# LayerNorm at the planner's lowest rank, its weight and bias folded into the transposed copy for the next layer, and another order of the first transfers

## The chip, the cores and the metric

The kernel runs on one core of one Trainium2 chip. The metric is the device time of one execution in microseconds (us); lower is better. The core has five engines that each work through an instruction queue of their own in order: TensorE (PE in the profile, with its weight loads as PEld), VectorE (DVE), ScalarE (ACT), GpSimd (POOL) and SyncE (SP, which here only issues DMAs). ACT issues a few DMAs too.

## The reference, cut to what matters

Two decoder layers over a sequence of 2048 tokens and 1024 channels, float32. Layer 0 mixes tokens with a gated delta rule (8 heads), layer 1 with gated linear attention (4 heads); each is followed by a residual and a LayerNorm:

```python
for i in range(DEPTH):                       # DEPTH = 2
    y = gdn_mixer(x, ...) if i % 2 == 0 else gla_mixer(x, ...)
    x = layer_norm(DEEP_ALPHA * x + y, ln_g[i], ln_b[i])

def layer_norm(x, g, b):
    mu = mean(x, -1); xc = x - mu; var = mean(xc * xc, -1)
    return xc * rsqrt(var + LN_EPS) * g + b
```

A mixer is an input projection (`x @ w_in`, 1024 by 6160 or by 3088), work per head and per chunk of tokens, a gated norm, and an output projection (`o @ w_out`, 2048 or 1024 by 1024). In layer 0 the gate and conv work is part of it. All products are wanted at float32 accuracy.

## The kernel before

**Tiling.** Tokens are cut into four groups of 512 (`TG`); a group is four tiles of 128 tokens (`NC = 4`, index n). A *unit* is one head of one layer for one group. `PHASES` gives the order of groups: layer 0 of groups 0 and 1, layer 1 of group 0, layer 0 of group 2, layer 1 of group 1, layer 0 of group 3, layer 1 of groups 2 and 3. That makes 48 units: eight for each of the four layer 0 groups (some 70 us each), four for each of the four layer 1 groups (some 55 us each).

**A unit's stages.** `gemms` multiplies the transposed input of the group (tiles xh, xl, read as xraw) with the unit's columns of the input weights; every float32 product is three fp32r products of high and low parts. `preps` does the work inside chunks, `chains` the recurrence over the four tiles, and `outs` multiplies the head's result (tiles oth, otl) with the output weights (tile wo) into PSUM buffer pso, of which there is one, and adds it to the residual: tile y, [128 tokens x 1024], with only four buffers, so one group's y at a time. After a group's last head `layer_norm` runs on each of the four y tiles: statistics on DVE (lnst, lnmv), the inverse root on POOL (lnrs), normalising on ACT (y<-y,lnmr,lnrs), multiplication with the weight on DVE and addition of the bias on POOL (both y<-y,gb), and a store, to x2 in layer 0 and to out in layer 1. In layer 0 the finished y is also transposed by PE (psg<-cst,y), copied from PSUM by ACT (xraw<-psg) and stored as x2T (x2T<-xraw, on ACT's queue); layer 1 later loads x2 as its residual (y<-x) and x2T as its transposed input (xraw<-x2T). The tile xraw has four buffers, shared between these loads and stores.

**Weights.** `chunk` brings one [128 x 256] piece of an input weight. At its first use it is loaded raw (wraw<-in_w_in), split in high and low part (wc; the high part by ACT, the low part by POOL), used, and the split pair is stored to DRAM (wk<-wc). At each later use the pair is loaded (wc<-wk). `load_wo` does the same for output weights (woraw, wo, wok), with ACT and DVE splitting. So the first eight units, and the first four of layer 1, load raw and store; all others only load.

**What sets the order.** Nothing runs as it is written. A `Recorder` notes every operation with its rank and unit. `place` then simulates the engines with a table of costs and lags, in which DMA issues are one more engine: whenever an engine is free it takes, of the operations that are ready by the simulation and whose buffers are free, the one with the lowest (rank, place in the program). Ranks before the change, first to last: `R_CHAIN`, `R_PREP`, `R_OUT`, `R_GEMM`, `R_SETUP`. An operation that needs a new buffer waits until its unit is at most two ahead of the first with an unfinished chain (`HORIZON`). The result is emitted as fixed instruction queues; on the chip each engine keeps that order, and an instruction whose data is late holds up all behind it. Since `emit` (line 356) issues everything, nearly every row of the profile says L356, and operations are told apart by tiles.

**Lines that the change touches.** `Recorder.cost` (a DMA issue is charged 430 ns on its queue, 520 for wc and wk), `chunk` and `load_wo`, `outs`, `load_gb` and `layer_norm`, the list of ranks, and the host's layout of inputs. In `outs` the loads of y and, through `load_wo`, of woraw have rank `R_OUT`, which stands ahead of `R_GEMM`:

```python
def outs(u):
    rec.rank = R_OUT
    if u.first:
        u.G["y"] = load_y(...)
```

Of the kernel before, what the change touches and what calls it, by code (L numbers as in the profile page):

```python
# [7 lines left out]
F32 = mybir.dt.float32  # L8
# [115 lines left out]
class Recorder:  # L124
# [53 lines left out]
    def cost(self, op, dst, every):  # L178
        key = op.key
        n = size_of(dst.shape)  # L180
        psum = any(isinstance(a, View) and a.of.psum for a in every)
        op.func = None
        if key == "t":
            mov = size_of(every[2].shape) if op.name == "matmul" else size_of(every[1].shape)
            if op.name == "transpose":
                op.cost = 2 * dst.shape[0] / 2.4 + 4
            elif every[1].dtype == F32:
                op.cost = 4 * mov / 2.4 + 9
            else:
                op.cost = mov / 2.25 + 4.5  # L190
            op.lag = 210
            op.func = op.name == "matmul" and min(dst.shape[0], every[1].shape[0]) < P
        elif key == "d":
            size = 4 * n * dst.shape[0]
            tag = dst.of.tag if isinstance(dst, View) else ""
            op.cost, op.lag = 520 if tag == "wc" or tag[:2] == "wk" else 430, DMA_LAG + size / 170
            if tag == "Arep":
                op.cost, op.lag = 620, REP_LAG
        elif key == "a":
            size = 4 * n * dst.shape[0]  # L200
            op.cost, op.lag = 340, DMA_LAG + size / 170
        elif key == "v":
            n = max(n, max(size_of(a.shape) for a in every))
            took = (150 if psum else 160) + 1.04 * n
            if op.name in ("tensor_reduce", "copy_predicated", "tensor_tensor_scan"):
                took += 1.0 * n
            if op.name != "tensor_tensor" and any(isinstance(a, (View, bass.AP)) and size_of(a.shape) == 1
                                                  for a in every[1:]):
                took += 62 if psum or n < 512 else 85
            op.cost, op.lag = took - 80, 80 + LAG  # L210
        elif key == "s":
            took = (165 if psum else 210) + 0.833 * n
            if any(isinstance(op.kw.get(k), (View, bass.AP)) for k in ("scale", "bias")):
                took += 100 + 67 * ("scale" in op.kw and "bias" in op.kw)
            if "accum_out" in op.kw:
                took += 190
            if op.name == "activation":
                op.func = "ln" if op.args[2] == AF.Ln else None if op.args[2] in (AF.Copy, AF.Square, AF.Identity,
                                                                                 AF.Abs) else "exp"
            op.cost, op.lag = took - 95, 95 + LAG  # L220
        else:
            took = 140 + 2.8 * n if len(every) > 2 else 185 + n
            if op.args[-1] == ALU.pow:
                took = 450 + 160 * n
            op.cost, op.lag = took - 40, 40 + LAG
# [148 lines left out]

@with_exitstack
def trunk(ctx, tc, x, xT, w_in1, conv, a_log, dt_bias, nw1, w_out1, w_in2, gk_up, gk_b, nw2, w_out2,
          ln_g, ln_b, consts, out, phases=None):
    nc = tc.nc
    rec = Recorder()
    v, s, g = (rec.engine(e, k) for e, k in ((nc.vector, "v"), (nc.scalar, "s"), (nc.gpsimd, "g")))  # L380
# [50 lines left out]
    nws = [T(f"nw{k}", [P, 2]) for k in range(2)]  # L431
    gkb = T("gkb", [P, H2])
    mhalf = T("mhalf", [P, NC])
    up = T("up", [80, 512], dt=F32R)
    halo = T("halo", [P, 32, 3])
    S1 = [T(f"S1_{h}", [P, DV]) for h in range(H1)]
# [22 lines left out]
    def setup_gla():  # L459
        sync.dma_start(nws[1][:], nw2)  # L460
        v.tensor_scalar(nws[1][:], nws[1][:], NORM, None, ALU.mult)
        sync.dma_start(gkb[:], gk_b)
        raw = T("th", [P, 512], 2)
        v.memset(raw[:], 0.0)
        for r0 in (0, 32, 64):
            sync.dma_start(raw[r0:r0 + 16, :], gk_up)
        s.copy(up[:], raw[:80, :])
        v.tensor_tensor(up[64:80, :], raw[64:80, :], up[64:80, :].bitcast(F32), ALU.subtract)
# [27 lines left out]
    def chunk(spec):  # L496


        w, cols, kc, key = spec
        wc = T("wc", [P, 2, 272], W_BUFS, F32R)  # L500
        n = sum(2 * cn if pair else cn for c0, cn, pair in cols)
        if key in kept:
            sync.dma_start(wc[:, :, :n].bitcast(F32), kept[key][:])
            return wc
        raw = T("wraw", [P, 272], RAW_BUFS)
        rows = w[kc * P:(kc + 1) * P]
        n = 0
        for c0, cn, pair in cols:
            if pair:
                sync.dma_start(raw[:, :2 * cn].rearrange("p (a b) -> p a b", a=2),  # L510
                               rows[:, :2 * pair].rearrange("p (a b) -> p a b", a=2)[:, :, c0:c0 + cn], also=(wc,))
                n = 2 * cn
            else:
                sync.dma_start(raw[:, n:n + cn], rows[:, c0:c0 + cn], also=(wc,) if n == 0 else ())
                n += cn
        split(wc[:, 0, :n], wc[:, 1, :n], raw[:, :n], g)
        kept[key] = T("wk", [P, 2, n], p=dr)
        sync.dma_start(kept[key][:], wc[:, :, :n].bitcast(F32))
        return wc

    def load_wo(spec, parts=None):
# [11 lines left out]
        if key in kept_wo:  # L533
            sync.dma_start(t[:].bitcast(F32), kept_wo[key][:])
        else:
            for j in range(2):
                raw = T("woraw", [P, 512], WO_RAW_BUFS)
                r0 = h * DV + j * P
                sync.dma_start(raw[:], w_out[r0:r0 + P, e * 512:(e + 1) * 512], also=(t,) if j == 0 else ())
                s.activation(t[:, j, 0, :], raw[:], AF.Copy, scale=nw[:, j:j + 1])  # L540
                v.scalar_tensor_tensor(t[:, j, 1, :], raw[:], nw[:, j:j + 1], t[:, j, 0, :].bitcast(F32),
                                       ALU.mult, ALU.subtract)
            kept_wo[key] = T("wok", [P, 2, 2, 512], p=dr)
            sync.dma_start(kept_wo[key][:], t[:].bitcast(F32))
# [461 lines left out]
    def outs(u):  # L1006
        rec.rank = R_OUT
        if u.first:
            u.G["y"] = load_y((lambda n: x[u.t0 + n * P:u.t0 + (n + 1) * P, :]) if u.kind == 0
                              else (lambda n: x2[u.gi][n][:]))  # L1010
        ys = u.G["y"]
        end = u.at + 1 == len(units)
        wo = {}
# [3 lines left out]
        for e, n in [(e, n) for n in range(NC) for e in range(2)] if end else [(e, n) for e in range(2) for n in range(NC)]:  # L1017
            final = u.last and e
            if e not in wo:
                wo[e] = load_wo(u.wo_specs()[e])  # L1020
            if final and not n and not end:
                gb = load_gb(u)
            c = slice(e * 512, (e + 1) * 512)
            d = PS("g" if u.at + 2 >= len(units) else "o", [P, 512])
            for j in range(2):
# [2 lines left out]
            y = ys[n]  # L1028
            v.scalar_tensor_tensor(y[:, c], d, u.z[:, n:n + 1], y[:, c], ALU.mult, ALU.add)
            if final:  # L1030
                layer_norm(u, n, y, gb)
        if u.last and u.kind == 0:
            for n in range(NC):
                for q in range(2):
                    d = PS("g", [P, 4, P])
                    transposes(d, lambda i: ys[n][:, (4 * q + i) * P:(4 * q + i + 1) * P], 4)
                    xt = T("xraw", [P, 4, P], X_RAW_BUFS)
                    s.copy(xt[:], d)
                    acts.dma_start(x2T[u.gi][:, 4 * q:4 * q + 4, n * P:(n + 1) * P], xt[:])

    def load_gb(u):
        gb = []
# [4 lines left out]
                gb.append(t)  # L1047
        return gb

    def layer_norm(u, n, y, gb):  # L1050
        st, mv = T("lnst", [P, 2, 6], 2), T("lnmv", [P, 2], 2)
        rs, mr = (small(k, 1, LN_BUFS) for k in ("lnrs", "lnmr"))
        for e in range(2):
            v.bn_stats(st[:, e, :], y[:, e * 512:(e + 1) * 512])
        v.bn_aggr(mv[:], flat(st[:]))
        rsqrt(rs[:], mv[:, 1:2], 1e-5 / ALPHA ** 2)
        v.scalar_tensor_tensor(mr[:], mv[:, 0:1], -1.0, rs[:], ALU.mult, ALU.mult)
        dst = x2[u.gi][n] if u.kind == 0 else out[u.t0 + n * P:u.t0 + (n + 1) * P, :]
        end = u.at + 1 == len(units)
        for e in range(2):  # L1060
            c = slice(e * 512, (e + 1) * 512)
            s.activation(y[:, c], y[:, c], AF.Identity, scale=rs[:], bias=mr[:])
            v.tensor_tensor(y[:, c], y[:, c], gb[e][:], ALU.mult)
            (v if end and n == NC - 1 else g).tensor_tensor(y[:, c], y[:, c], gb[2 + e][:], ALU.add)
            sync.dma_start(dst[:, c], y[:, c])

    for u in units:
# [10 lines left out]
WO_BUFS, WO_RAW_BUFS = 2, 2  # L1078
LN_BUFS = 4
N_WARM = 5  # L1080
R_CHAIN, R_PREP, R_OUT, R_GEMM, R_SETUP = range(5)
HORIZON = 2
LAGS_C = (0, 3)
LAGS_T = (0, 3, 8, 11)
# [3 lines left out]
def host_layout(np, i):  # L1088
# [15 lines left out]
        "w_out2": f(np.asarray(i["gla_w_out"])[0]),  # L1104
        "ln_g": f(np.asarray(i["ln_g"])),
        "ln_b": f(np.asarray(i["ln_b"])),
        "consts": shape_constants(np),
    }

# [16 lines left out]
```

## Time and profile before

| what | us |
|---|---|
| median of 3 runs | 3136.71 (3135.39 to 3137.48) |
| the profiled execution, its own time | 3134.49 |
| span of that execution, first to last instruction | 3132.6 |
| PE busy | 3026.9 (97%) |
| DVE busy | 2041.2 (65%) |
| ACT busy | 1174.5 (37%) |
| POOL busy | 520.1 (17%) |
| granted TensorE clock, mean | 0.987 |

The profile lists one execution. A row of the timeline or of the groups gives the engine, the operation, the tile it writes and those it reads (out<-in), shapes, and how often (x4). A timeline row begins with start and duration; its bracket holds the idle time of the engine ahead of it and what ended that. A row of the windows view is one stretch of time: the busy time of each engine with its count of instructions, the granted clock of PE, the share of the DMA engines and GB/s. Times that the texts call span plus 1.9 us (3134.49 less 3132.6) are the profiled execution's own.

### The profile page before, as it was taken

The page shows a single profiled execution, that of the slowest core. Times are in us where ns is not written, and L with a number is a line of the kernel's source. Part 1 is how long each engine was busy: PE and PEld are TensorE (multiplying, and loading weights), DVE is VectorE, ACT ScalarE, POOL GpSimd, SP SyncE. Part 2 cuts the span into 40 slices and gives each one's busy share as a digit, 9 for nine tenths or more (in the row PEclk, how much of TensorE's full clock was granted, in tenths as well). Part 3 has the DMA queues.
Part 4 walks back from the last instruction along what each step waited for, and adds up shares of the span by engine and source line. Part 5 has one row for each costly group of instructions (what it writes and reads, how often), then busy time and mean ns, then how long its engine had stood idle before and what let it go on. Part 6 is the DMA issues. An engine that isn't in the chain of part 4 may idle for free.

```text
span 3132.6 us, 51373 instructions
## 1 busy us (share of the span) xinstructions
PE 3026.9 (97%) x18430; PEld 2592.1 (83%) x18430; DVE 2041.2 (65%) x4780; ACT 1174.5 (37%) x3091; POOL 520.1 (17%) x834
## 2 busy tenths in 40 slices
PE   7999999999999989999999999999999999999997
PEld 5788888788888878888888888998888889889886
DVE  5777777766666675576675667447666666646645
ACT  4544444433223454443332344323333334423422
POOL 3433332200000243320000002002000000201001
PEclk9999999999999999999999999999999999999999
DMA  8766567654555558674445445547444544655542
GB/s 268 222 194 216 179 213 232 190 169 125 153 176 155 177 182 265 208 234 151 128 145 177 145 157 188 162 157 238 137 142 141 156 147 146 212 172 180 175 142 91
DMA packets 442479, 551.85 MB, mean 176 GB/s; under 512 B 37568, under 2 KB 381888, under 8 KB 430192
## 3 DMA queue, kind: packets, MB, share of 16 engines
q1 hardware_dynamic: 416112, 530.74, 53.6%
q10 hardware_dynamic: 26112, 17.83, 2.0%
q8 instruction: 145, 2.38, 0.3%
q14 instruction: 110, 0.90, 0.1%
HBM read 421.24 MB, written 127.21 MB: 175 GB/s over the span
## 4 chain that ended last, share of the span: by engine, by line
PE 80%; DVE 9%; DMA 5%; ACT 3%; issue 2%; POOL 1%; SPq 1%; ACTq 0%; DVEq 0%; POOLq 0%
PE psg L356 45%; PE psc L356 15%; PE pso L356 14%; PE psh L356 6%; DMA wraw<-in_w_in 2%; DVE y L356 2%; DVE acc L356 1%; ACT junk L356 1%; DVE D L356 1%; SPq L356 1%; POOL wc L356 1%; DMA x2T<-xraw 1%; DVE lnst L356 1%; DVE kd L356 1%; DVE Xt L356 0%
## 5 line engine op out<-in xcount | busy, mean ns | idle before, releaser
L356 PE MATMUL psg<-xh,wc 128*128 128x512 f32 x2560 | 902.4, 416 | 13.8 <-ACT xh L356 7.3
L356 PE MATMUL psg<-wc,xh 128*128 128x256 f32 (+1 forms) x4096 | 809.1, 290 | 19.5 <-ACT wc L356 13.1
L356 PEld LDWEIGHTS psg<-wc,xh 128*128 128x128 f32 x4096 | 656.4, 190 | 45.2 <-ACT wc L356 15.2
L356 PE MATMUL psg<-wc,xl 128*128 128x256 f32 (+1 forms) x2048 | 589.5, 290 | 0.0
L356 PEld LDWEIGHTS psg<-xh,wc 128*128 128x128 f32 x2560 | 480.8, 190 | 112.2 <-ACT xh L356 9.1
L356 PE MATMUL psg<-xl,wc 128*128 128x512 f32 x1280 | 532.9, 417 | 0.5 <-DVE xl L356 0.5
L356 PE MATMUL pso<-wo,oth 128*128 128x512 f32 x1472 | 477.0, 403 | 17.1 <-DVE y L356 16.3
L356 DVE SCALAR_TENSOR_TENSOR y<-pso,z,y 128x512 f32<-128x512 f32 x368 | 274.4, 746 | 194.4 <-PE pso L356 171.5
L356 PEld LDWEIGHTS psg<-wc,xl 128*128 128x128 f32 x2048 | 388.8, 191 | 7.1
L356 DVE SCALAR_TENSOR_TENSOR acc<-pb,taps,acc 128x512 f32<-128x512 f32 x384 | 300.0, 785 | 77.8 <-ACT acc L356 71.5
L356 PEld LDWEIGHTS pso<-wo,oth 128*128 128x128 f32 x1472 | 260.2, 189 | 75.8 <-DVE y L356 28.4
L356 POOL TENSOR_TENSOR wc<-wraw,wc 128x256 fp32r<-128x256 f32 (+1 forms) x288 | 233.2, 824 | 417.4 <-ACT wc L356 388.5
L356 PE MATMUL pso<-wo,otl 128*128 128x512 f32 x736 | 295.4, 401 | 0.1
L356 PEld LDWEIGHTS psg<-xl,wc 128*128 128x128 f32 x1280 | 243.2, 190 | 48.1 <-DVE xl L356 1.9
L356 ACT ACTIVATE th<-psg 128x256 f32<-128x256 f32 (+1 forms) x256 | 108.8, 437 | 447.2 <-PE psg L356 419.4
L356 ACT ACTIVATE junk<-psc 128x128 bf16<-128x128 f32 (+1 forms) x448 | 144.4, 322 | 226.4 <-PE psc L356 125.2
L356 POOL COPY halo<-pb 128x3 f32<-128x3 f32 x128 | 29.2, 228 | 902.3 <-ACT pb L356 900.0
L356 ACT COPY pb<-psg 128x512 f32<-128x512 f32 x128 | 74.9, 585 | 250.7 <-PE psg L356 237.7
L356 PEld LDWEIGHTS pso<-wo,otl 128*128 128x128 f32 x736 | 139.3, 189 | 30.6 <-DVE otl L356 0.9
L356 DVE SCALAR_TENSOR_TENSOR sg<-th,psg 128x256 f32<-128x256 f32 x192 | 79.9, 416 | 125.8 <-ACT th L356 111.6
L356 ACT CAST wc<-wraw 128x256 fp32r<-128x256 f32 (+1 forms) x288 | 110.0, 406 | 122.9 <-DMA wraw<-in_w_in 104.0
L356 ACT ACTIVATE D<-D 128x512 f32<-128x512 f32 x160 | 99.2, 630 | 115.5 <-DVE D L356 108.1
(171 smaller groups left out, 4391.4 us busy)
## 6 DMA issues: line engine op xcount, KB each, us to landing
wc<-wk SPq DMA_DIRECT2D x816, 256.0 KB, 3.5
wo<-wok SPq DMA_DIRECT2D x70, 1024.0 KB, 4.9
wk<-wc SPq DMA_DIRECT2D x272, 256.0 KB, 3.5
wraw<-in_w_in SPq DMA_DIRECT2D x288, 128.0 KB, 3.7
wok<-wo SPq DMA_DIRECT2D x24, 1024.0 KB, 6.1
Arep<-blk SPq DMA_DIRECT2D x32, 512.0 KB
wc<-wk SPq DMA_DIRECT2D x48, 272.0 KB, 3.2
woraw<-in_w_out SPq DMA_DIRECT2D x48, 256.0 KB, 4.4
```

What stands on the lines that cost most here:

```text
L356: tc.keep_in_program_order(op.call(*[real(a) for a in op.args], **{k: real(a) for k, a in op.kw.items()}))
```

## The change

1. A new rank `R_LN` stands between `R_GEMM` and `R_SETUP`. `layer_norm`, the loads of weight and bias (`load_gb`) and the new `affine` get it, but for the very last unit, where they keep `R_OUT`.
2. `layer_norm` now ends with the normalised y. Multiplication with the weight, addition of the bias and the store move to `affine`. In layer 1 it follows directly. In layer 0 the transposes read the y that is only normalised, and ACT applies weight and bias, which in the transposed tile are one number per partition (new input ln_T, tile lnT), in the copy from PSUM; `affine` on y follows behind the transposes.
3. The transposes of a group are ordered by channel block: four transposes (one per token tile, last tile first) fill one PSUM tile, and the store to x2T writes 512 consecutive tokens per partition rather than four blocks of 128.
4. The bias is added by DVE instead of POOL, but for the first three tiles of the last unit.
5. Loads of y get rank `R_GEMM` (`R_SETUP` in the first unit), those of woraw too.
6. The split input weights of the first two units (`N_UNKEPT = 2`) are not stored; the first two heads of the second group load them raw, split them again and store them.
7. The planner charges 480 ns for a DMA issue (630 for wc and wk, 560 for wraw, 720 for Arep), and 9500 ns until a load of y has landed.

```diff
@@ Recorder.cost
-            op.cost, op.lag = 520 if tag == "wc" or tag[:2] == "wk" else 430, DMA_LAG + size / 170
+            op.cost, op.lag = 630 if tag == "wc" or tag[:2] == "wk" else 560 if tag == "wraw" else 480, DMA_LAG + size / 170
             if tag == "Arep":
-                op.cost, op.lag = 620, REP_LAG
+                op.cost, op.lag = 720, REP_LAG
+            elif tag == "y":
+                op.lag = 9500
@@ setup_gla
+        sync.dma_start(lnT[:], ln_T)
@@ chunk
+        keep = rec.unit >= N_UNKEPT
...
-        kept[key] = T("wk", [P, 2, n], p=dr)
-        sync.dma_start(kept[key][:], wc[:, :, :n].bitcast(F32))
+        if keep:
+            kept[key] = T("wk", [P, 2, n], p=dr)
+            sync.dma_start(kept[key][:], wc[:, :, :n].bitcast(F32))
@@ load_wo
             for j in range(2):
+                rec.rank = R_GEMM if rec.unit else R_SETUP
                 raw = T("woraw", [P, 512], WO_RAW_BUFS)
                 r0 = h * DV + j * P
                 sync.dma_start(raw[:], w_out[r0:r0 + P, e * 512:(e + 1) * 512], also=(t,) if j == 0 else ())
+                rec.rank = R_OUT
@@ outs
         if u.first:
+            rec.rank = R_GEMM if u.at else R_SETUP
             u.G["y"] = load_y(...)
+            rec.rank = R_OUT
...
             if final and not n and not end:
+                rec.rank = R_LN
                 gb = load_gb(u)
+                rec.rank = R_OUT
...
             if final:
-                layer_norm(u, n, y, gb)
+                if not end:
+                    rec.rank = R_LN
+                layer_norm(u, n, y)
+                if u.kind:
+                    affine(u, n, y, gb)
+                rec.rank = R_OUT
         if u.last and u.kind == 0:
+            for kc in range(KC):
+                d = PS("g", [P, NC, P])
+                for n in reversed(range(NC)):
+                    pe.transpose(d[:, n, :], ys[n][:, kc * P:(kc + 1) * P], ident)
+                xt = T("xraw", [P, TG], X_RAW_BUFS)
+                s.activation(xt[:], flat(d), AF.Identity, scale=lnT[:, kc:kc + 1], bias=lnT[:, KC + kc:KC + kc + 1])
+                acts.dma_start(x2T[u.gi][:, kc, :], xt[:])
+            rec.rank = R_LN
             for n in range(NC):
-                for q in range(2):
-                    d = PS("g", [P, 4, P])
-                    transposes(d, lambda i: ys[n][:, (4 * q + i) * P:(4 * q + i + 1) * P], 4)
-                    xt = T("xraw", [P, 4, P], X_RAW_BUFS)
-                    s.copy(xt[:], d)
-                    acts.dma_start(x2T[u.gi][:, 4 * q:4 * q + 4, n * P:(n + 1) * P], xt[:])
+                affine(u, n, ys[n], gb)
@@ layer_norm
+        for e in range(2):
+            c = slice(e * 512, (e + 1) * 512)
+            s.activation(y[:, c], y[:, c], AF.Identity, scale=rs[:], bias=mr[:])
+
+    def affine(u, n, y, gb):
         dst = x2[u.gi][n] if u.kind == 0 else out[u.t0 + n * P:u.t0 + (n + 1) * P, :]
         end = u.at + 1 == len(units)
         for e in range(2):
             c = slice(e * 512, (e + 1) * 512)
-            s.activation(y[:, c], y[:, c], AF.Identity, scale=rs[:], bias=mr[:])
             v.tensor_tensor(y[:, c], y[:, c], gb[e][:], ALU.mult)
-            (v if end and n == NC - 1 else g).tensor_tensor(y[:, c], y[:, c], gb[2 + e][:], ALU.add)
+            (g if end and n < NC - 1 else v).tensor_tensor(y[:, c], y[:, c], gb[2 + e][:], ALU.add)
             sync.dma_start(dst[:, c], y[:, c])
@@ constants
+N_UNKEPT = 2
-R_CHAIN, R_PREP, R_OUT, R_GEMM, R_SETUP = range(5)
+R_CHAIN, R_PREP, R_OUT, R_GEMM, R_LN, R_SETUP = range(6)
```

More of the change, by code (lines that the diff above doesn't have):

```diff
@@ L376, in trunk @@
 def trunk(ctx, tc, x, xT, w_in1, conv, a_log, dt_bias, nw1, w_out1, w_in2, gk_up, gk_b, nw2, w_out2,
-          ln_g, ln_b, consts, out, phases=None):
+          ln_g, ln_b, ln_T, consts, out, phases=None):
     nc = tc.nc
@@ L433, in trunk @@
     mhalf = T("mhalf", [P, NC])
+    lnT = T("lnT", [P, 2 * KC])
     up = T("up", [80, 512], dt=F32R)
@@ L1048, in load_gb, with layer_norm @@
         return gb
-    def layer_norm(u, n, y, gb):
+    def layer_norm(u, n, y):
         st, mv = T("lnst", [P, 2, 6], 2), T("lnmv", [P, 2], 2)
@@ L1106, in host_layout @@
         "ln_b": f(np.asarray(i["ln_b"])),
+        "ln_T": f(np.stack([np.asarray(i["ln_g"])[0], np.asarray(i["ln_b"])[0]]).reshape(2 * KC, P).T),
         "consts": shape_constants(np),
```

## The prediction, made before the changed kernel was run

> **What bounds the kernel now.** I read the page first, for the busiest engine, then the windows in steps of 40 us, for where that engine rests, then the waits in the worst of them.
>
> ```profile
> span 3132.6 us, 51373 instructions
> PE 3026.9 (97%) x18430; PEld 2592.1 (83%) x18430; DVE 2041.2 (65%) x4780; ACT 1174.5 (37%) x3091; POOL 520.1 (17%) x834
> ```
>
> PE rests 3132.6 - 3026.9 = 105.7 us. Its work is not changed (the transposes are as many as before), so the change can win only these rests and what hangs on them. Columns below: stretch; PE, PEld, DVE, ACT, POOL busy (and instructions); PE's granted clock; DMA share; GB/s.
>
> ```profile
> 0.00:40.00 40.00, 25.99 (x89) 17.86 (x90) 20.06 (x39) 16.55 (x33) 11.95 (x21) 0.87 0.88 296
> 40.00:80.00 40.00, 32.40 (x168) 26.73 (x168) 21.49 (x48) 16.64 (x59) 20.53 (x28) 0.96 0.78 244
> 80.00:120.00 40.00, 37.43 (x201) 31.88 (x199) 34.74 (x74) 19.20 (x45) 22.76 (x32) 0.96 0.80 243
> 160.00:200.00 40.00, 39.52 (x264) 33.82 (x265) 25.75 (x75) 16.85 (x56) 11.75 (x19) 1.00 0.67 218
> ...
> 600.00:640.00 40.00, 34.70 (x208) 27.48 (x207) 34.48 (x76) 18.19 (x33) 16.87 (x22) 1.00 0.93 299
> 640.00:680.00 40.00, 39.94 (x238) 35.02 (x237) 27.72 (x80) 13.06 (x45) 2.66 (x5) 1.00 0.42 127
> ...
> 1120.00:1160.00 40.00, 33.79 (x195) 28.10 (x192) 35.03 (x59) 25.59 (x53) 24.51 (x26) 0.99 0.53 173
> 1160.00:1200.00 40.00, 32.61 (x199) 28.84 (x199) 20.26 (x45) 15.11 (x34) 6.16 (x8) 0.84 0.81 261
> ...
> 1360.00:1400.00 40.00, 36.49 (x153) 29.27 (x152) 30.98 (x73) 16.44 (x44) 17.21 (x23) 0.91 0.88 281
> ...
> 1920.00:1960.00 40.00, 35.13 (x216) 30.45 (x215) 24.13 (x45) 14.91 (x29) 7.07 (x5) 0.91 0.71 230
> ...
> 2120.00:2160.00 40.00, 36.56 (x155) 29.34 (x155) 30.84 (x73) 16.44 (x44) 17.95 (x23) 0.91 0.83 278
> ...
> 2680.00:2720.00 40.00, 34.89 (x216) 30.17 (x215) 23.80 (x45) 14.57 (x29) 8.02 (x7) 0.91 0.72 241
> ...
> 2880.00:2920.00 40.00, 37.24 (x238) 32.14 (x237) 32.23 (x65) 20.00 (x37) 14.35 (x13) 0.96 0.79 254
> ```
>
> The reader is to see that the rests lie together: at the start and at the seven places where a group ends in LayerNorm. A low clock follows each long rest and costs again; as its price I take 40 us times (1 - clock), an upper bound, since part of it falls on the rest itself. Rest plus clock:
>
> - start, three rows: 14.0 + 7.6 + 2.6 = 24.2 of rest, 5.2 + 1.6 + 1.6 = 8.4 of clock: 32.6
> - 600: 5.3
> - 1120 and 1160: 13.6 + 6.8 = 20.4
> - 1360 and 2120: 6.9 + 7.2 = 14.1
> - 1920 and 2680: 10.0 + 7.2 = 17.2
> - 2880: 2.8 + 1.6 = 4.4
>
> That is 94.0 in all, and 61.4 of it at the seven LayerNorms.
>
> **The start.** SP's issues (first three) and PE's first real product:
>
> ```profile
> 0.72 1.81 SPq L356 DMA_DIRECT2D y<-in_x  x4
> 2.58 0.95 SPq L356 DMA_DIRECT2D woraw<-in_w_out  x2
> 3.57 0.45 SPq L356 DMA_DIRECT2D xraw<-in_xT  x1
> ...
> 12.33 1.22 PE L356 MATMUL psg<-xh,wc 128*128 128x512 f32 x2 [6.32 <-ACT xh L356]
> ```
>
> Six DMAs that nobody needs for tens of us are issued ahead of the first input, 2.5 MB (4 x 512 KB, 2 x 256 KB). At the 296 GB/s of the first row they take 8.4 us. The new ranks put them behind: the first xraw goes out at 0.72 rather than 3.57 (2.85 us) and then has the DMA engines to itself. The head's gain lies between 2.85 and the whole wait of 6.32; I take 5.5, nearer the upper end, because the 8.4 us of transfer in front go too. These y and woraw loads, the constants and the new lnT (128 x 16 numbers, one more small DMA) still go out in unit 0, later.
>
> The other 24.2 - 6.3 = 17.9 us of rest up to 120 us are small waits, mostly for raw weights that arrive late at DMA shares of 0.78 to 0.88. The first two units lose their 48 stores (24 chunks each), 256 KB apiece: 12.6 MB of the 31.3 MB that the three rows moved (40 us x 296 + 244 + 243 GB/s). SP also saves 48 issues. Bounds: nothing, and 17.9. I take 7, since part waits for DVE or ACT in the first convolutions. With the rests, of 8.4 us of clock I take 3.5. Start: -16 (bounds -3 and -30).
>
> The price: two heads of the second group are loaded raw, split and stored again. Row 160 is such a stretch (first group), row 640 one that only loads; PE differs by 0.42 us in 40, so 140 us cost 1.5. I take +2.
>
> **LayerNorm.** What POOL's bias does, at the second group's end (timeline; then the groups):
>
> ```profile
> 1149.04 5.57 DVE L356 TENSOR_TENSOR y<-y,gb 128x512 f32<-128x512 f32 x4 [0.21 <-ACT y L356]
> 1150.63 6.77 POOL L356 TENSOR_TENSOR y<-y,gb 128x512 f32<-128x512 f32 x4
> 1154.53 3.41 DVE L356 SCALAR_TENSOR_TENSOR wo<-woraw,nw,wo 128x512 fp32r<-128x512 f32 x2
> 1159.78 1.09 PE L356 MATMUL psg<-cst,y 128*128 128x128 f32 x4 [5.40 <-POOL wc L356]
> ```
> ```profile
> L356 POOL TENSOR_TENSOR y<-y,gb 128x512 f32<-128x512 f32 x62 | 94.9, 1550 | 26.4 <-DVE y L356 13.2 <-PE psg L356 6.1 <-issue 4.1
> L356 DVE TENSOR_TENSOR y<-y,gb 128x512 f32<-128x512 f32 x66 | 57.6, 898 | 1.1 <-ACT y L356 0.8
> L356 DVE SCALAR_TENSOR_TENSOR wo<-woraw,nw,wo 128x512 fp32r<-128x512 f32 x48 | 39.3, 833 | 3.9 <-ACT wo L356 3.9
> L356 ACT ACTIVATE y<-y,lnmr,lnrs 128x512 f32<-128x512 f32 x64 | 48.1, 807 | 55.1 <-DVE lnmr L356 54.7
> L356 ACT COPY xraw<-psg 128x512 f32<-128x512 f32 x32 | 18.5, 583 | 12.3 <-PE psg L356 10.5 <-DMA wc<-wk 1.2 <-ACT th L356 0.4
> ```
>
> Beside POOL's additions DVE's own work stretches: 1.39 us a multiplication (5.57 / 4) against 0.90 in the mean, 1.70 us a wo product (3.41 / 2) against 0.83. So DVE and POOL run late together, and PE's transposes, which read the finished y, stand 5.40 us. After the change they read the normalised y, and the chain through weight, POOL and bias is gone from PE's path.
>
> What is added: 56 of the 62 additions go to DVE (6 of the last unit stay on POOL), at the 0.90 of a multiplication +50 us; DVE is busy 65%, and at lowest rank they go where it rests (19.7 us in row 1160, 12.3 in row 640), so nothing on the path; without that cover a LayerNorm's eight would cost 7.2. ACT's 32 copies take weight and bias: 807 against 583, +0.22 each, 7 us in all, under ACT's 37%. A burst is new: eight copies follow the last normalisation with four xraw buffers, and a late store holds ACT, and all behind it, up. It has four places, each with a wait of 0 to 5.2 us (the landing of x2T below); the rows of now hold few such waits (12.3 us of ACT ahead of 32 copies), so I take a quarter of 5.2 each: +5, bounds 0 and 21.
>
> What moves on SP: per group eight stores of y and four loads of gb, behind the weight loads in rank. SP waits in order, and today it stands for POOL's y:
>
> ```profile
> SPq L356 <- POOL y L356: 54.3, 23, 15.6
> ```
>
> That is 54.3 us in 23 waits, at most 15.6, and the next weights stand behind. Eleven wc buffers cover it: each buffer feeds 12 products, and at row 640's pace (40 us / 238 = 0.17 us a product, others included) that is 2 us a buffer, 22 in all. After the change SP waits for DVE's y in the same places, with the same cover: 0.
>
> ```profile
> 1162.67 9.97 DMA x2T<-xraw
> ```
> ```profile
> 1172.71 0.33 SPq L356 DMA_DIRECT2D gb<-in_ln_b  x1
> ...
> 1173.61 0.89 SPq L356 DMA_DIRECT2D wraw<-in_w_in  x1
> ...
> 1177.81 0.58 PE L356 MATMUL psg<-wc,xh 128*128 128x256 f32 x1 [4.86 <-ACT wc L356]
> ```
>
> The second stall there starts on the chain with one x2T store that took 9.97 us; SP's next issue stands behind it, the raw weights behind that, and PE 4.86 us. New x2T rows are 2 KB in one piece instead of 512 bytes, gb and y loads rank lower, and SP's costs are charged higher. The store should land between the 3.5 us of an equal wk<-wc and the 5.2 of now. I take half of 20.4: -11, bounds 0 and -20.
>
> ```profile
> wk<-wc SPq DMA_DIRECT2D x272, 256.0 KB, 3.5
> ...
> x2T<-xraw ACTq DMA_DIRECT2D x32, 256.0 KB, 5.2
> ...
> y<-x SPq DMA_DIRECT2D x16, 512.0 KB, 5.4
> ```
> ```profile
> 1945.15 0.75 DVE L356 SCALAR_TENSOR_TENSOR y<-pso,z,y 128x512 f32<-128x512 f32 x1 [6.10 <-DMA y<-x]
> ```
>
> At 1945 (and alike in row 2680) DVE waits 6.10 us for layer 1's residual, PE behind it for the one pso buffer. The planner is now told 9.5 us rather than 6.6 (3500 + 524288 / 170 ns) for that load, so it should put the products later and other PE work ahead: -9 of 17.2, bounds 0 and -17. Stretch 600 has no clock loss and small waits; -1. At 1360 and 2120 PE waits 3.1 us each for the logits of the next group, made on DVE in the middle of a LayerNorm with 12 us of POOL additions beside it; lower rank helps some: -3 of 14.1. At 2880, 0.
>
> The last unit keeps its order: 0. Elsewhere the new DMA costs shuffle the order: 0, bounds -4 and +4.
>
> Sum: -16 + 2 - 11 + 5 - 9 - 1 - 3 = -33. On the profiled execution 3134.5 - 33 = 3101.5; the median lies 2.2 above it (3136.7 - 3134.5), so 3103.7, **I say 3104**.
>
> **A rule against it.** The Trainium skill, "SBUF — State Buffer", section "Who interferes with whom", says that a DVE instruction with two SBUF inputs shares a read port with a GpSimd instruction that reads SBUF, and one blocks the other. The stretched rows at 1149 and 1154 agree. By that rule the additions stay exposed on DVE, now to POOL's weight splits; it is the first rival.
>
> **The rivals.**
> - *DVE late beside POOL's splits.* Where raw weights are split during a LayerNorm (600, newly, and 1120 to 1200), 16 multiplications and additions stretch from 0.90 to 1.39: 8 us each, 16 us, and the gains there (1 and 11) go with them. If half of the 16 reaches PE: -33 + 12 + 8 = -13, 3124. For it: DVE was full (34.5 and 35.0 of 40) there. Against: a split takes POOL little time in the row 640 kind of stretch, and the lowest rank steps aside.
> - *Rank moves nothing.* Ranks only choose among ready work; where DVE rests LayerNorm comes as early as ever, and each stall is replaced by another of its size. Then the start alone counts: -16 + 2 = -14, 3123.
> - *The residual comes later still: slower.* Finished y now needs 16 DVE passes (14 us at 0.90) behind the last transpose, at lowest rank, then a store and a load (5.4 us each); four y buffers only. If the next unit's output products are in PE's queue before that, each of the seven ends stalls PE for these passes, 14 us, the clock counted in: 98 against 61.4, +37, less 14 for the start: 3160. It decides once the seven average above (61.4 + 14) / 7 = 10.8 us. Against: the planner sees these lags and has a unit of 50 us to fill with.
> - *All of it.* Half of what the forecast leaves of the 94.0 goes too, (94 - 40) / 2 = 27: 3077.
>
> **How the numbers follow.** Forecast 0.55 (its own range 3086 to 3116); the two small gains 0.27 together; all of it 0.06; slower 0.07; a shuffle that eats the start's gain, 3131 to 3143, 0.05. A measurement of this kernel can tell about 0.2%, 6.3 us. Faster 0.88, same 0.05, slower 0.07. The range 3083 to 3132 leaves out the last two and most of "all of it": 0.17.
>
> **What would show it.** The first product at 6 to 7.5 us; rest below 17 us up to 120 us; no POOL row y<-y,gb but for the last unit, and DVE's y<-y,gb near 0.65 us; x2T landing under 5.2 us; the 4.86 and both y<-x waits gone. I am wrong if the start keeps its 24 us, or if the windows of the seven ends still hold over 50 us.

## The result, and the profile after

The changed kernel takes 3086.33 us (median of 4 runs, 3077.73 to 3094.14) against 3136.14 (3135.39 to 3137.48): a ratio of 0.984, 95% interval 0.9812 to 0.9868, 49.8 us less. Run a second time beside other kernels it gave 3086.17 (3083.14 to 3088.75), ratio 0.9843 (0.9828 to 0.9858). The forecast was 3104, with a range of 3083 to 3132 and a range of its own of 3086 to 3116: right in sign and inside the range, but 33 us of gain were forecast and 50 came.

The profiled execution is the shortest of the four, 3077.73 us, 8.6 under the median; against the profiled one of before it is 56.8 us shorter. The head of its page:

```profile
span 3075.7 us, 51507 instructions
PE 3006.5 (98%) x18430; PEld 2577.9 (84%) x18430; DVE 2048.6 (67%) x4836; ACT 1195.1 (39%) x3139; POOL 480.0 (16%) x826
```

PE has the same 18430 products. Its rest fell from 105.7 to 3075.7 - 3006.5 = 69.2 us, and its busy time fell by 20.4 us too: fewer products ran at the halved clock (mean granted clock 0.995 against 0.987). The windows of the same places, some 35 us earlier in the later half of the span (columns as in the prediction):

```profile
0.00:40.00 40.00, 34.53 (x171) 26.74 (x172) 26.17 (x51) 20.92 (x51) 19.74 (x28) 1.00 0.80 252
40.00:80.00 40.00, 37.38 (x176) 29.97 (x175) 34.06 (x68) 24.48 (x69) 24.25 (x39) 1.00 0.50 143
80.00:120.00 40.00, 37.18 (x246) 31.35 (x245) 28.79 (x63) 18.66 (x64) 20.34 (x27) 0.96 0.49 148
...
520.00:560.00 40.00, 37.57 (x215) 32.16 (x214) 22.20 (x56) 17.79 (x61) 14.10 (x22) 0.87 0.67 205
560.00:600.00 40.00, 38.15 (x179) 29.62 (x178) 36.86 (x81) 23.54 (x55) 15.76 (x30) 1.00 0.67 207
600.00:640.00 40.00, 34.96 (x229) 29.61 (x228) 32.17 (x70) 20.24 (x59) 17.20 (x21) 0.91 0.86 286
...
1120.00:1160.00 40.00, 37.33 (x263) 32.97 (x262) 30.80 (x61) 25.86 (x56) 15.34 (x20) 1.00 0.85 289
1160.00:1200.00 40.00, 39.22 (x226) 33.56 (x226) 22.51 (x41) 19.82 (x46) 13.40 (x18) 1.00 0.86 283
...
1320.00:1360.00 40.00, 38.28 (x193) 32.04 (x192) 32.23 (x81) 16.71 (x43) 6.96 (x17) 1.00 0.88 298
...
1880.00:1920.00 40.00, 38.62 (x270) 34.07 (x269) 28.76 (x61) 19.45 (x39) 1.28 (x2) 1.00 0.74 258
...
2080.00:2120.00 40.00, 38.31 (x179) 31.07 (x178) 34.69 (x92) 17.09 (x48) 5.51 (x15) 1.00 0.89 300
...
2640.00:2680.00 40.00, 39.30 (x268) 35.06 (x269) 28.28 (x62) 17.63 (x35) 0.00 (x0) 1.00 0.86 286
```

The start kept 5.5 + 2.6 + 2.8 = 10.9 us of rest and 1.6 of clock: 12.5 against 32.6. The ends at 1140, 1340, 1890, 2100 and 2650 lost nearly all their rest and, with it, all of the low clock: 3.5, 1.7, 1.4, 1.7 and 0.7 us, together 9.0, against 20.4 + 14.1 + 17.2 = 51.7. The first end, at 600, got worse: 1.9 + 5.0 of rest and 3.6 of clock against 5.3. The head of the timeline, SP's first issue and PE's first real product:

```profile
0.72 0.40 SPq L358 DMA_DIRECT2D xraw<-in_xT  x1
...
5.25 0.73 PE L358 MATMUL psg<-xh,wc 128*128 128x512 f32 x2
```

It starts at 5.25 us instead of 12.33, with no rest ahead of it. The groups of LayerNorm and the DMA table (us to landing last):

```profile
L358 DVE TENSOR_TENSOR y<-y,gb 128x512 f32<-128x512 f32 x122 | 86.7, 738 | 8.7 <-PE psg L358 7.8 <-ACT y L358 0.6
L358 ACT ACTIVATE xraw<-psg,lnT 128x512 f32<-128x512 f32 x32 | 23.8, 780 | 8.7 <-DMA wk<-wc 4.7 <-PE psg L358 1.9 <-DVE X L358 1.2
...
L358 POOL TENSOR_TENSOR y<-y,gb 128x512 f32<-128x512 f32 x6 | 9.7, 1637 | 3.0 <-DVE lnmv L358 2.5 <-DVE lnmr L358 0.4
```
```profile
x2T<-xraw ACTq DMA_DIRECT2D x32, 256.0 KB, 4.4
...
y<-x SPq DMA_DIRECT2D x16, 512.0 KB, 6.6
```

122 instructions of DVE on y now take 86.7 us where 66 took 57.6: 56 more for 29 us more, since one takes 738 ns instead of 898. PE's waits for the out-projection's buffer, 16.3 us before, are down to this:

```profile
PE pso L358 <- DVE y L358: 4.8, 13, 1.2
```

The new kernel's times spread over 16 us. They go with the mean granted clock: 3077.73 us at 0.995, 3083.51 at 0.993, 3089.15 at 0.992, 3094.14 at 0.991. A clock of 0.004 less over 3085 us is 12 us.

### The profile page after: what moved, and what is told of

It is laid out like the page before. It is cut to its first block, busy times and chain, and to the rows that moved or that the text cites. A ratio compares the mean times of both kernels' runs of the same rounds, so it can differ in the third digit from the quotient of the medians.

```text
span 3075.7 us, 51507 instructions
## 1 busy us (share of the span) xinstructions
PE 3006.5 (98%) x18430; PEld 2577.9 (84%) x18430; DVE 2048.6 (67%) x4836; ACT 1195.1 (39%) x3139; POOL 480.0 (16%) x826
## 4 chain that ended last, share of the span: by engine, by line
PE 84%; DVE 7%; DMA 4%; ACT 2%; issue 2%; SPq 1%; POOL 0%; ACTq 0%; DVEq 0%; POOLq 0%
PE psg L358 48%; PE psc L358 16%; PE pso L358 15%; PE psh L358 6%; DMA wraw<-in_w_in 1%; DVE acc L358 1%; DVE y L358 1%; DVE D L358 1%; ACT junk L358 1%; DMA wc<-wk 1%; DVE kd L358 1%; SPq L358 1%; DVE Xt L358 0%; DMA Gb<-gcT 0%; DMA wk<-wc 0%
## 5 line engine op out<-in xcount | busy, mean ns | idle before, releaser
L358 PE MATMUL psg<-xh,wc 128*128 128x512 f32 x2560 | 892.5, 412 | 4.5 <-ACT xh L358 2.3
L358 PE MATMUL psg<-wc,xh 128*128 128x256 f32 (+1 forms) x4096 | 809.1, 290 | 10.9 <-ACT wc L358 3.4
L358 PE MATMUL pso<-wo,oth 128*128 128x512 f32 x1472 | 469.1, 399 | 4.9 <-DVE y L358 4.8
L358 POOL TENSOR_TENSOR wc<-wraw,wc 128x256 fp32r<-128x256 f32 (+1 forms) x336 | 281.2, 852 | 428.7 <-ACT wc L358 377.9
L358 ACT CAST wc<-wraw 128x256 fp32r<-128x256 f32 (+1 forms) x336 | 128.4, 406 | 81.2 <-DMA wraw<-in_w_in 66.1
```

Of the source, the lines that this page charges most:

```text
L358: tc.keep_in_program_order(op.call(*[real(a) for a in op.args], **{k: real(a) for k, a in op.kw.items()}))
```

## The experiments

The theory, "stalls by place": the start gave its own part, and the LayerNorm ends gave the rest because POOL's bias left PE's path. The rivals: "truer DMA costs" (the planner's new numbers set the order right, wherever it helped), and "rank moves nothing". Kernels with a_ are the changed one with a part undone, those with b_ the one before with a part done. Each was timed beside the kernel before; a ratio difference of 0.001 is 3.1 us. The intervals reach some 0.0015 each way, so two ratios must differ by about 0.002, 6 us, before the runs can tell them apart.

To see where each one gains, I took from every trace the rest of PE plus half of the time at half clock, by place: the start (to 120 us), and each group's end from 20 us ahead of its first statistics (lnst) to 45 us behind the last. "Logits" are the ends at 1360 and 2120 of before, "residual" those at 1930 and 2700.

| kernel (one trace each) | start | end at 600 | end at 1140 | logits | residual | elsewhere, with 2880 | last unit | median us, ratio |
|---|---|---|---|---|---|---|---|---|
| before | 32.7 | 5.9 | 21.1 | 13.7 | 17.2 | 27.8 | 26.6 | 3136.1 |
| changed | 12.6 | 10.3 | 3.3 | 3.4 | 3.4 | 27.1 | 25.6 | 3086.3, 0.9840 |
| changed, second trace | 13.0 | 12.6 | 3.2 | 3.5 | 3.4 | 26.0 | 27.4 | 3086.2, 0.9843 |
| b_new_start | 18.3 | 9.9 | 19.4 | 12.2 | 15.1 | 27.9 | 27.9 | 3124.0, 0.9976 |
| b_new_costs | 30.9 | 6.2 | 22.1 | 12.1 | 12.8 | 28.5 | 26.6 | 3124.4, 0.9977 |
| b_dve_bias | 32.6 | 7.6 | 16.8 | 16.1 | 2.1 | 23.1 | 27.4 | 3119.8, 0.9955 |
| b_three | 14.3 | 17.9 | 20.5 | 8.4 | 0.0 | 25.9 | 26.4 | 3098.5, 0.9884 |
| a_old_start | 37.1 | 8.1 | 2.7 | 5.3 | 3.4 | 28.5 | 27.9 | 3097.9, 0.9894 |
| a_old_costs | 17.0 | 10.6 | 6.5 | 6.2 | 0.4 | 25.9 | 28.2 | 3089.4, 0.9866 |
| a_pool_bias | 13.2 | 18.9 | 9.1 | 6.5 | 11.3 | 34.6 | 27.4 | 3116.6, 0.9953 |
| a_old_transposes | 14.8 | 7.0 | 11.0 | 5.1 | 1.7 | 33.7 | 27.1 | 3083.7, 0.9844 |
| a_rank_out | 13.1 | 8.7 | 3.5 | 12.1 | 0.7 | 24.3 | 27.1 | 3082.6, 0.9840 |
| a_keep_all | 18.8 | 8.6 | 2.3 | 8.7 | 3.5 | 24.1 | 26.0 | 3088.1, 0.9848 |
| a_best | 10.3 | 4.4 | 4.1 | 6.4 | 3.4 | 22.8 | 24.0 | 3078.6, 0.9827 |

A row holds one execution, and executions of one kernel differ by up to 16 us; the ratios decide, the places explain. The two rows of the changed kernel differ by up to 2.3 us in a column. The traces of a_old_transposes (3092.46 us) and a_old_start (3103.40) are the slowest executions of their kernels, 8.8 and 5.5 us above the median.

**The start.**

```diff
 a_old_start (from the changed kernel)
-N_UNKEPT = 2
+N_UNKEPT = 0
-                rec.rank = R_GEMM if rec.unit else R_SETUP     (woraw, in load_wo)
-            rec.rank = R_GEMM if u.at else R_SETUP             (y, in outs)
```

> The changed kernel (3086) with the three start edits undone: y and woraw loads again at R_OUT, and the split weights of the first two units stored as before. Theory 'stalls by place' (the start gave its own part, the LayerNorm ends the rest): rest up to 120 us back from 10.9 to over 20 us, the seven ends keep their gain, time 3100 to 3110. Rival 'truer DMA costs' (the planner's new issue costs and the 9.5 us for y set the order right wherever it helped): the planner then works round the early loads, rest up to 120 us under 15, time 3084 to 3092.

3097.92 us, ratio 0.9894 (0.988 to 0.9909): 16 to 17 us of the gain go, a little under the expected time. The theory's place is right: the start is back at 37.1, the ends stay good.

> The kernel before (3136) with the start edits alone: y loads at R_GEMM (R_SETUP in the first unit), woraw likewise, the split weights of the first two units not stored. Theory 'stalls by place': rest up to 120 us falls from 24 to about 11, clock loss there from 8 to 2, two heads are split twice; 3114 to 3122. Rival 'truer DMA costs': under half of that, 3126 to 3136.

The same edits put into the kernel before: 3123.98 us, 0.9976 (0.9964 to 0.9987), a gain of 8 us, between theory and rival. The start gained 14.4 in its trace, but the end at 600, where two heads are now split twice while POOL adds the bias, lost 4.0, and the medians kept less than the one trace shows.

```diff
 a_keep_all (from the changed kernel)
-N_UNKEPT = 2
+N_UNKEPT = 0
```

> The changed kernel with the first two units' split weights stored again and not split a second time (loads of y and woraw stay late). Theory 'stores crowd the start': rest up to 120 us rises from 11 to 17 or more, the end of the first group (rest and clock 10 us) falls to 5, 3085 to 3095. Rival 'the early loads were the whole of it': the start keeps its 11 us and the second split is saved, 3076 to 3084.

3088.10 us, 0.9848 (0.9834 to 0.9863), against 0.9843 beside it: no difference that this can tell. Both halves of the theory are seen in the traces and cancel in part: with the stores back the start loses 18.8 - 12.6 = 6.2 and the end at 600 gains 1.7 (5.8 and 4.0 against the second trace), less than the theory had. So leaving out the stores gives no time that these runs can tell; by difference from a_old_start, the start's gain in time hangs on the late loads of y and woraw. No run undoes these alone.

**The bias on DVE.**

```diff
 a_pool_bias (from the changed kernel); b_dve_bias is the reverse, put into the one before
-            (g if end and n < NC - 1 else v).tensor_tensor(y[:, c], y[:, c], gb[2 + e][:], ALU.add)
+            (v if end and n == NC - 1 else g).tensor_tensor(y[:, c], y[:, c], gb[2 + e][:], ALU.add)
```

> The changed kernel (3086) with the bias added by POOL again. Theory 'stalls by place': most of the gain at the ends was POOL's additions leaving; they stretch DVE again (y<-y,gb multiplications over 0.85 us, wo products too) and late LayerNorms bring stalls back, 3095 to 3110. Rival 'off the path': since transposes now read the normalised y, nothing on PE's path waits for the bias, whichever engine adds it; 3080 to 3090.

> The kernel before (3136) with the bias added by DVE, nothing else. Theory 'stalls by place': the 5.40 us in front of the transposes near 1159 and the stretched DVE rows go, some of the later ones too; 3112 to 3126. Rival 'off the path': DVE has 50 us more to do in its fullest stretches and the transposes still wait for the finished y; 3130 to 3145.

Undone: 3116.55 us, 0.9953 (0.9938 to 0.9968); 34 us of the 50 go, more than the theory gave it. Alone: 3119.79, 0.9955 (0.9938 to 0.9972), 12 to 14 us, in the expected range, though not where I had put it: the stall at 1155 shrank little (21.1 to 16.8), while both residual waits went (17.2 to 2.1). By its times "off the path" falls twice. In a_pool_bias DVE's rows on y are the slowest of all:

```profile
L358 DVE TENSOR_TENSOR y<-y,gb 128x512 f32<-128x512 f32 x66 | 61.9, 954 | 3.9 <-ACT y L358 2.3 <-PE psg L358 1.4
```

954 ns against 738 without POOL beside them. No product of PE waits for the bias there, yet the end at 600 costs 18.9 us: what PE waits for is other work that runs late, above all the buffer of a copy to x2T:

```profile
606.17 1.11 PE L358 MATMUL psg<-cst,y 128*128 128x128 f32 x4 [5.30 <-ACT xraw L358]
```

The 5.40 us ahead of the transposes at 1159.78 in the kernel before, which the prediction gave to the bias, were mostly of this kind too. The bracket of that row names a weight split on POOL (wc), not a bias. POOL's last addition ended at 1150.63 + 6.77 = 1157.40, and PE stood 2.4 us longer, until ACT had copied the transposes ahead of these out of their psg buffer, of which there are three. ACT in turn had stood for raw weights:

```profile
1158.23 0.40 ACT L356 CAST wc<-wraw 128x256 fp32r<-128x256 f32 x1 [5.39 <-DMA wraw<-in_w_in]
...
1159.06 0.58 ACT L356 COPY xraw<-psg 128x512 f32<-128x512 f32 x1
```

So the bias can have held PE there for at most 3.0 of the 5.40 us, which fits the 16.8 of 21.1 us that b_dve_bias leaves at this end. How POOL's additions cost PE elsewhere is not separated. They stretch DVE; and SP stands for the y that they finish, 61.6 us in a_pool_bias against 20.6 in the changed kernel (for DVE's y 14.7 and 34.4), with loads queued behind. No run changes the one without the other.

**The planner's DMA costs.**

```diff
 a_old_costs (from the changed kernel); b_new_costs is the reverse, put into the one before
-            op.cost, op.lag = 630 if tag == "wc" or tag[:2] == "wk" else 560 if tag == "wraw" else 480, DMA_LAG + size / 170
+            op.cost, op.lag = 520 if tag == "wc" or tag[:2] == "wk" else 430, DMA_LAG + size / 170
...
-                op.cost, op.lag = 720, REP_LAG
-            elif tag == "y":
-                op.lag = 9500
+                op.cost, op.lag = 620, REP_LAG
```

> The changed kernel (3086) with the planner's old DMA costs (430, 520, 620 ns; no 9.5 us for y). Theory 'stalls by place': only the two waits for layer 1's residual (about 17 us with the clock in the kernel before) hang on them, 3090 to 3103. Rival 'truer DMA costs': most of the 50 us is lost, over 3110.

> The kernel before (3136) with the planner's new DMA costs alone. Theory 'stalls by place': the two waits for layer 1's residual shrink, the rest stays; 3120 to 3132. Rival 'truer DMA costs': 3090 to 3110.

Undone: 3089.42 us, 0.9866 (0.9851 to 0.988), some 7 us; alone: 3124.41, 0.9977 (0.9965 to 0.9989), some 7 us. The rival "truer DMA costs" is out. But where the 7 us lie is not where I had them. PE's waits in b_new_costs:

```profile
PE psg L358 <- ACT xraw L358: 14.0, 7, 5.1
...
PE pso L358 <- DVE y L358: 5.2, 15, 0.9
```

The wait for the residual does go when the planner expects the load late (16.3 to 5.2 us). In its place the transposes wait for ACT's copies: 3.5 us before (8.9 with the 5.40 us at 1159), 14.0 now, some of it at the same ends (1.33 and 1.98 us ahead of two transposes at 1911 and 1914). So the residual column falls by 4.4 only. With the bias on DVE the same waits are gone whether the planner knows the lag or not (a_old_costs 0.4).

**Rank and fold.**

```diff
 a_rank_out (from the changed kernel)
-R_CHAIN, R_PREP, R_OUT, R_GEMM, R_LN, R_SETUP = range(6)
+R_CHAIN, R_PREP, R_OUT, R_GEMM, R_SETUP = range(5)
+R_LN = R_OUT
 a_old_transposes (from the changed kernel): affine follows layer_norm in layer 0 as well, then
...
             for n in range(NC):
-                affine(u, n, ys[n], gb)
+                for q in range(2):
+                    d = PS("g", [P, 4, P])
+                    transposes(d, lambda i: ys[n][:, (4 * q + i) * P:(4 * q + i + 1) * P], 4)
+                    xt = T("xraw", [P, 4, P], X_RAW_BUFS)
+                    s.copy(xt[:], d)
+                    acts.dma_start(x2T[u.gi][:, 4 * q:4 * q + 4, n * P:(n + 1) * P], xt[:])
```

> The changed kernel (3086) with LayerNorm, affine and the loads of weight and bias at R_OUT, where they were. Theory 'stalls by place': the lowest rank is a minor part, as ranks only choose among ready work; 3084 to 3096. Rival 'rank is the change' (the logits of the next group and the weight splits get DVE and ACT first): the stalls for the logits at 1320 and 2080 come back with their clock, over 3100.

3082.57 us, 0.984 (0.9822 to 0.9857): the same as with the lowest rank. The logits column does come back, 12.1 against 3.4, but not the rival's stalls: no product of PE waits for the logits (6.2 us before), and the long rests are two waits for ACT (junk), this one and one of 3.02 us at 2111:

```profile
1359.61 2.08 PE L358 MATMUL psc<-kq 128*128 128x256 f32 x4 [3.41 <-ACT junk L358]
```

Over all columns a_rank_out has 89.5 us, the two traces of the changed kernel 85.7 and 89.1: what comes back there is less elsewhere.

> The changed kernel (3086) where the transposes again read the finished y, in the old order (per token tile, 512-byte rows to x2T), with plain copies; ranks, DVE's bias, costs and start stay. Theory 'stalls by place': weight and bias stand before the transposes again, now at lowest rank, so x2T comes later but is needed only 200 us later; some of the stalls at 600, 1140 and 1890 come back: 3088 to 3100. Rival 'rank moves nothing': the same 3084 to 3090, with x2T landing at 5.2 us instead of 4.4. Third: the fold alone carried the gain of the ends, over 3105.

3083.70 us, 0.9844 (0.9827 to 0.986): the same again. Here items 2 and 3 of the change, called the fold below, are both undone; no run takes them apart. So the two parts that name this change can each be taken out at no cost that the runs can tell. Taking out both is another matter:

```diff
 b_three (from the kernel before): the edits of b_new_start, b_new_costs and b_dve_bias together
```

> The kernel before with three of the edits together: the start (loads of y and woraw, no stores of the first two units' split weights), the planner's new DMA costs, and the bias on DVE; LayerNorm keeps its rank R_OUT and the transposes read the finished y. Alone these three gave about 8, 7 and 14 us. Theory 'rank and fold are worth nothing': 3080 to 3090, as with all edits. Rival 'parts add up': 8 + 7 + 14 = 29 us, 3102 to 3109. Third, 'rank and fold stand in for each other': either is enough beside the three and none is not; again 3100 or more, with a stall of over 10 us (clock counted) left at the second group's end, near 1140.

3098.47 us, 0.9884 (0.9865 to 0.9903): more than the 29 us of the parts, but 13 us short of the changed kernel. "Rank and fold are worth nothing" (3080 to 3090) is out. The third theory has its sign, the end at 1140 keeps 20.5 us, though the time is 1.5 us under its 3100. What stands there, from the chain of waits, SP's issues and PE's rows of b_three:

```profile
1156.87 10.26 DMA x2T<-xraw
```
```profile
1167.15 0.84 SPq L358 DMA_DIRECT2D wraw<-in_w_in  x2
```
```profile
1171.06 0.58 PE L358 MATMUL psg<-wc,xh 128*128 128x256 f32 x1 [9.09 <-ACT wc L358]
```

It is the stall of before in the same form: one x2T store is under way for 10.26 us; SP issues other DMAs meanwhile, but then stands 2.3 us for an earlier x2T store and 2.3 us for this one, the raw weights behind go out only at 1167.15, ACT cannot split, and PE rests 9.09 us. SP's waits for such stores, in b_three, before, and in the changed kernel:

```profile
SPq L358 <- DMA x2T<-xraw: 28.2, 15, 3.5
```
```profile
SPq L356 <- DMA x2T<-xraw: 19.3, 10, 5.2
```
```profile
SPq L358 <- DMA x2T<-xraw: 2.9, 2, 2.4
```

With fold and rank, 28.2 us become 2.9. With the fold alone (a_rank_out) they are 0.4 us and the end at 1140 costs 3.5, with the rank alone (a_old_transposes) 15.4 and 11.0. So the four, with the start and the costs as in the changed kernel: bias on POOL with rank and fold 0.9953, about what start and costs give alone (0.9976 x 0.9977 = 0.9953); bias on DVE with neither 0.9884; with the rank 0.9844; with the fold 0.984; with both 0.984 and 0.9843. With DVE's bias rank and fold are worth 13 us, and either will do. Without it they look worth nothing; that supposes that gains multiply, for no run has start and costs alone, and the three of b_three did not quite (0.9908 by the parts, 0.9884 measured).

**A version that goes on from here.**

```diff
 a_best (from the changed kernel)
-N_UNKEPT = 2
+N_UNKEPT = 1
-            (g if end and n < NC - 1 else v).tensor_tensor(y[:, c], y[:, c], gb[2 + e][:], ALU.add)
+            (g if end and n < NC - 2 else v).tensor_tensor(y[:, c], y[:, c], gb[2 + e][:], ALU.add)
```

> The changed kernel, with stores left out for one unit instead of two, and in the last unit the bias of the third token tile on DVE instead of POOL. In the last 19 us POOL's additions stretch DVE (eight y<-y,gb in 9.3 us); with two fewer the tail should shorten by 1 to 2 us. One head fewer is split twice: 1 to 4 us at the first group's end, against 0 to 3 at the start. Expected 3078 to 3088, the tail 1 to 2 us shorter.

> The changed kernel itself, beside the other three, as what they are compared with. Its four times spread from 3077.7 to 3094.1, those of the kernel before over 2 us. Theory 'short stalls near the clock's threshold': the spread comes with the mean granted clock (0.991 to 0.995) and is there again, ratio 0.982 to 0.987. Rival 'one odd execution': all within 4 us.

a_best: 3078.56 us (3073.97 to 3086.39), 0.9827 (0.9807 to 0.9848); the changed kernel beside it 0.9843 (0.9828 to 0.9858). It clearly beats the kernel before; against the changed one the intervals overlap. The tail is where it can be seen, in DVE's last rows of the changed kernel and of a_best:

```profile
3062.58 8.57 DVE L358 TENSOR_TENSOR y<-y,gb 128x512 f32<-128x512 f32 x7
```
```profile
3061.38 7.65 DVE L358 TENSOR_TENSOR y<-y,gb 128x512 f32<-128x512 f32 x9
```

Nine instructions with two of POOL's additions beside them (0.85 us each) are done sooner than seven with four (1.22 each). The last unit's column falls by 1.6, but the two traces of the changed kernel differ there by 1.8. The end at 600 shows 4.4 with one head split twice, against 10.3 and 12.6 with two and 8.6 with none, so this is not the splitting alone. The second set of runs of the changed kernel spread by 5.6 us with clocks of 0.992 to 0.995, not by 16 nor within 4: the spread is there again, smaller, and follows the clock only roughly (3086.71 us at 0.992, 3088.75 at 0.993).

## Why the prediction was right, and where it was not

- *The bound.* PE's rests and the clock behind them were all there was to win: their sum fell by 59.2 us in the table (145.0 to 85.8), the span by 56.9. Counting the clock with the rest was needed; 20.4 us of the gain are busy time of PE.
- *The start, -16.* The two profiles show -20.1, taking it out cost 16 to 17 us. The head gave 7.1 us, more than the 6.3 that I had as its upper bound. The 7 of the small waits, most of it from the stores left out, shows as 6.2 at the start, partly paid back at 600, and as no time that can be told. The re-splitting, +2, shows as 1.7 and 4.0. Two slips of the working change nothing: the upper bounds of the start add up to 32.6, not 30, and 4 x 512 and 2 x 256 KB are 2.6 million bytes, 8.9 us at that rate.
- *The ends, -24 and +5 for the burst.* The profiles give -41 for the seven (61.4 to 9.0 + 10.5 + 0.5 in the 40 us windows, the last at 2840). This is the mis-sized term. Each end was priced at half or less, as though a part of the stall would come back; at five of them nothing came back, and the low clock went with the rest. The burst's +5 did not happen: PE waits 3.8 us in all for ACT's copies (8.9 before, with the 5.40 at 1159). They do not come as a burst: at the second group's end the eight lie between 1129.7 and 1144.0.
- *What removes them.* "The bias leaves PE's path" was not the mechanism. At most 3.0 of the 5.40 us were the bias's, and a_pool_bias, where no product of PE waits for it, still loses 34 us. What counts is that POOL does not do the additions; that the time fell inside the range although this step was wrong is in part luck. b_dve_bias shows the bias on DVE alone at the residual waits, where I had put the gain down to the planner's 9.5 us; at 1140 it takes the fold or the rank as well, since the second stall there, SP behind a slow x2T store, is the larger one. I read that stall from the chain rightly and still gave it to three edits at once without asking which.
- *The residual waits, -9.* Wrong step: the planner's lag moves the wait to the transposes' copies (14.0 us in b_new_costs). DVE's bias ends both.
- *Rank.* "Rank moves nothing" had a chance as a rival for the whole; for the rank itself it was right. Its -3 at the logits was the wrong step: the waits for the logits are gone with it and without it.
- *The rule against it.* "DVE late beside POOL's splits" has its place: of the seven ends only the one at 600, where POOL now splits again, got worse (5.3 to 10.5). But without those splits it still costs 8.6 (a_keep_all), so they explain a small part. At 1120 to 1200, where POOL splits as before, nothing of it is seen.
- *The slower rival.* The residual came no later for PE: 4.8 us of waits for y, against 16.3. "All of it" (3077) was nearer to the result than its chance of 0.06 says; the median lies 9 us above it and 18 below the forecast.

What stays open: by which way POOL's additions cost PE; and what makes the end at 600 worse, in nearly every kernel with the new start. In both traces of the changed kernel PE's longest rest there is for DVE's U, 2.15 and 3.49 us, so DVE is late, but no run shows why.

## What to carry to other kernels

A stall on a busy engine costs its length and the low clock behind it, so ask for each what removes all of it, not half. Where several queues meet in one stall, undo the edits in pairs: here two of them stood in for each other, and each alone looked worthless. An engine with spare time is not a free place for work if it slows its neighbour: POOL's additions cost DVE a quarter more per instruction (898 and 954 ns against 738), and PE then stood for work that does not read them, whether through DVE or through SP's queue. And see when the instruction that a bracket names had ended, and what else ended just then: the stall that I gave to the bias was ended by a copy.

## What the runs showed of the hardware that I had not expected

Rests of PE much shorter than the 4.5 to 5.4 us ones are followed by half clock, but not always. In the changed kernel's profile a rest of 2.31 us at 521 was followed by some 10 us of it (clock 0.87 in the window from 520), while the same rest in the second trace of the same kernel, 2.33 us at 524, was followed by none, nor was that in a_rank_out, 2.20 us at 522 (the windows of these two):

```profile
520.00:560.00 40.00, 37.35 (x238) 31.26 (x236) 26.08 (x65) 19.65 (x65) 16.12 (x24) 1.00 0.73 228
```
```profile
520.00:560.00 40.00, 37.47 (x231) 31.08 (x231) 26.24 (x66) 19.85 (x66) 15.90 (x24) 1.00 0.72 219
```

So the same queues can run with and without that loss, and times go with the clock: the changed kernel spread by 16 and by 6 us, the one before by 2 in its first set and by 6 to 10 in later ones (3139.63 us at a clock of 0.986, 3129.47 at 0.989).

A store of 256 KB whose landing is 4 to 5 us in the median can take 10 (9.97 and 10.26 us, both x2T beside loads of y, gb and weights), and SP's queue can then stand (5.2 us in the kernel before), though the next issue reads and writes nothing of it. The trace of before gives the reason: that issue, the load of gb at 1172.71, is counted on the same semaphore as the x2T store of 1162.67 and waits for it first; eight such semaphores take turns over the DMAs of both queues.
